# The reciprocal root of the norms on GpSimd instead of VectorE, in a hybrid encoder block on one core

## The chip, the cores and the metric

The kernel runs on one core of one Trainium2 chip. The metric is the device time of one execution in microseconds (us); lower is better. A core has five engines that run side by side, each with its own queue that is worked off in order: TensorE (PE in the profile; PEld is its loading of weights), VectorE (DVE), ScalarE (ACT), GpSimd (POOL) and SyncE (SP, which here only issues DMAs). They wait for each other through semaphores.

## The reference, cut to what matters

One layer of a streaming encoder on a sequence of 256 tokens with 1024 channels, all in float32:

```
x <- x + 1/2 * rmsnorm(swiglu(rmsnorm(x)))          first FFN, 2816 wide
h  = rmsnorm(x);  p = h @ w_in                      one projection, split into
A  = HGRN2 recurrence (8 heads), then rmsnorm and an output gate
B  = forgetting attention (8 heads, causal)
y  = gate_A * (A @ w_branch_a) + gate_B * (B @ w_branch_b)
x <- x + rmsnorm(y @ w_out)
x <- x + rmsnorm(cross_attention(rmsnorm(x), rmsnorm(mem)))     4 heads, 256 memory rows
x <- x + 1/2 * rmsnorm(swiglu(rmsnorm(x)))          second FFN

def rmsnorm(x, g):
    y = x * rsqrt(mean(x * x, axis=-1) + EPS)
    return y * g
```

What matters here is the `rsqrt` in `rmsnorm`: one number for each token, ten norms, each over two halves of 128 tokens.

## The kernel before, in words

The 256 tokens are two halves `h` of 128, one token to a partition. All matrix products keep float32 precision by splitting each operand into a high part `hi` (rounded to the format that TensorE takes) and a low part `lo`, and adding three products. The weights are 260 units of 128 x 1024. For each unit (function `unit`, lines 118 to 120) SP loads `raw`, ScalarE makes `hi` (L119) and VectorE makes `lo = raw - hi` (L120). There are 4 buffers for `raw` and 8 each for `hi` and `lo`, so the units are prepared ahead of their use. Every product is recorded by the helper `MM`, so all of them have line L78.

A norm is computed in three steps. ScalarE sums the squares of a row in two halves of 512 columns (`ssq`, L235). `rstd_of` turns the two sums into the reciprocal root. It does so without a table: a first value from the bits of the number taken as an integer (L221), then three Newton steps of two instructions (L224 and L226), and, if `scaled`, a last factor (L231). All its operands are 128 x 1. The result is then used in one of these ways:

- `post` adds a normed output to `x`. For one half: `ssq` on the two PSUM banks, L292 (the bank times the gain, into `post`), `rstd_of` without the last factor, and L296 (`xs = post * root + xs`). In the last FFN the two DMAs of the output half follow.
- `half` transposes the new `x` of a half for the next stage (`to_T`: transposes on PE at L269, then ScalarE L260 and VectorE L261), and calls `rstd_x`, which gives the root of the new `x`. The root is applied later, after the product, so PE need not wait for it.
- `row_of` makes a row of 256 roots: VectorE multiplies the identity with the root (L252, `diag`), PE multiplies it with ones, ScalarE copies the row (L255). VectorE then multiplies product banks with that row (L307 and L309 in the FFNs).
- The root of a half is also a factor in L443, L601, L602, L641, L729, L315, L317 and others.

`rstd_of` is called 20 times: two for each of the five norms on entry to a stage (four of `x`, one of `mem`), two for the norm behind HGRN2 (L641 uses it), and eight in `post`.

The order of the work on each engine is set when the program is built: a planner orders the instructions by priority, from the order in which they are written and from its own costs. `after(i)` gives a block a high priority and queues its instructions behind the `i`-th product. The constants L_F1, L_IA, L_WO, L_MK, L_MO and L_F2 place the transposes of `half` in this way.

GpSimd does little: the identity, some memsets, two selects (L651), and the DMAs of L208, L210, L467, L645 and L649 in its queue.

Of the kernel before, what the change touches and what calls it, by code (L numbers as in the profile page):

```python
# [11 lines left out]
I32 = mybir.dt.int32  # L12
AF = mybir.ActivationFunctionType
ALU = mybir.AluOpType
# [3 lines left out]
D = 1024  # L18
# [5 lines left out]
EPS = 1e-6  # L24
# [39 lines left out]
def block_kernel(ctx: ExitStack, tc: tile.TileContext, wts, x_in, xT_in, mem_in, memT_in, cols, rows, fbias, masks, out):  # L64
    nc = tc.nc
    V, S, G, PE = nc.vector, nc.scalar, nc.gpsimd, nc.tensor
# [21 lines left out]
    def nm(s):  # L88
        count[0] += 1
        return f"{s}_{count[0]}"  # L90

    def m4(shape, dt=F32, n="m"):
        return mp.tile(shape, dt, tag="m4", name=nm(n))

    def s1(n=1, dt=F32, name="s"):
        return sp.tile([P, n], dt, tag=f"s{n}", name=nm(name), bufs=16)
# [119 lines left out]
    def rstd_of(s, scaled=True):  # L216

        v = s1(name="v")
        V.tensor_scalar(out=v, in0=s[:, 0:1], scalar1=s[:, 1:2], scalar2=D * EPS, op0=ALU.add, op1=ALU.add)
        y = s1(name="y")  # L220
        V.tensor_scalar(out=y.bitcast(I32), in0=v.bitcast(I32), scalar1=-0.5, scalar2=1597463007.0, op0=ALU.mult, op1=ALU.add)  # L221
        for c in (3.0, 12.0, 768.0):
            t = s1(name="t")
            V.scalar_tensor_tensor(out=t, in0=v, scalar=y, in1=y, op0=ALU.mult, op1=ALU.mult)  # L224
            y2 = s1(name="y")
            V.scalar_tensor_tensor(out=y2, in0=t, scalar=c, in1=y, op0=ALU.subtract, op1=ALU.mult)  # L226
            y = y2
        if not scaled:
            return y
        r = s1(name="rstd")  # L230
        V.tensor_scalar(out=r, in0=y, scalar1=-1.0 / 256.0, scalar2=None, op0=ALU.mult)  # L231
        return r

    def ssq(dst, src):
# [2 lines left out]
    def rstd_x(src):  # L237

        s = s1(2, name="ss2")
        for j in range(2):  # L240
            ssq(s[:, j : j + 1], src[j])
        return rstd_of(s)
# [42 lines left out]
    def post(ps, h, grow, factor=1.0, last=False):  # L285

        s = s1(2, name="ss2")
        ts = []
        for j in range(2):
            ssq(s[:, j : j + 1], ps[j])  # L290
            t = sp.tile([P, 512], F32, tag="z2", name=nm("post"), bufs=3)
            V.scalar_tensor_tensor(out=t, in0=ps[j], scalar=-factor / 256.0, in1=grow[:, j * 512 : (j + 1) * 512], op0=ALU.mult, op1=ALU.mult)  # L292
            ts.append(t)
        r = rstd_of(s, scaled=False)
        for j, (t, xh) in enumerate(zip(ts, x_halves(h))):
            V.scalar_tensor_tensor(out=xh, in0=t, scalar=r, in1=xh, op0=ALU.mult, op1=ALU.add)  # L296
            if last:
                nc.sync.dma_start(out[h * P : (h + 1) * P, j * 512 : (j + 1) * 512], xh)
# [307 lines left out]
    for c in range(2):  # L606
        for name, lst, sc in (("k_b", kb_, 1.0), ("q_b", qb_, 1.0 / math.sqrt(128.0))):
            u = chunk(name, c)
            t = m4([P, 4, T], n=name)
# [20 lines left out]
    for h in range(2):  # L630
# [8 lines left out]
        r = rstd_x(ps)  # L639
# [7 lines left out]
    for g in range(2):  # L647
        t = m4([P, 4, T], n="cbm")
# [74 lines left out]
    for c in range(2):  # L723
        u = chunk("v_b", c)
        t = m4([P, 2, 512], n="v_b")
# [86 lines left out]
    for c in range(2):  # L812
        u = chunk("mk", c)
        KM.more()
        for j in range(2):
            js = slice(2 * j, 2 * j + 2)
            ps = proj_col2(M, u, (2 * j, 2 * j + 1))
            t = sp.tile([P, 2, T], F32, tag="z2", name=nm("km"), bufs=3)
# [171 lines left out]
```

## Time and profile before

| what | us |
|---|---|
| median of three runs | 815.56 |
| lowest and highest of them | 814.79 and 817.03 |
| the profiled execution | 814.88 |
| its span in the profile | 813.1 |
| TensorE busy | 799.4 |
| VectorE busy | 538.7 |
| ScalarE busy | 409.7 |
| GpSimd busy | 10.2 |

The span runs from the first to the last recorded instruction. The time of the profiled execution is 1.8 us longer, for what lies around the span. The granted clock of TensorE was 0.998 of full speed. Times within the kernel are given from the start of the span. A line of the timeline reads: start, length, engine, source line, operation, output and inputs with their shapes, count, and in brackets the idle time of the engine before it and what ended that.

### The profile page before, as it was taken

To read this page: it belongs to the slowest core of one execution; us is meant where nothing else is said; L and a number is where in the kernel's file an instruction comes from. 1 tells how busy PE (TensorE), PEld (TensorE's weight loads), DVE (VectorE), ACT (ScalarE), POOL (GpSimd) and SP (SyncE) were. 2 spreads that over 40 slices of the span, in tenths; PEclk is the share of its full clock that TensorE was granted. 3 is DMA by queue.
4 is the path that set the end of the run, shared out by engine and by line. 5 is a ranking of instruction groups with operands and counts; after the bars stand their busy time and mean duration, and the time that the engine had idled before them with its cause. 6 is when DMAs were issued, how large, how long until landed. Compare 5 with 4: busy or idle time off the path is not lost.

```text
span 813.1 us, 15302 instructions
## 1 busy us (share of the span) xinstructions
PE 799.4 (98%) x6292; PEld 743.5 (91%) x6292; DVE 538.7 (66%) x866; ACT 409.7 (50%) x621; POOL 10.2 (1%) x22
## 2 busy tenths in 40 slices
PE   8999999999999999999999999999999999999996
PEld 8999999997799889998999998999887899999994
DVE  6964666468776896678585556975748654665454
ACT  7644544436664435348675335744647544444431
POOL 0000000000000100100000000000000000000000
PEclk9999999999999999999999999999999999999999
DMA  8874466464564454543477446456426664566421
GB/s 322 256 264 156 163 207 226 157 207 160 171 208 170 149 193 161 198 152 121 139 231 243 150 168 220 156 179 203 143 83 197 208 207 156 164 212 227 149 104 52
DMA packets 41093, 147.02 MB, mean 181 GB/s; under 512 B 4744, under 2 KB 4752, under 8 KB 41024
## 3 DMA queue, kind: packets, MB, share of 16 engines
q1 hardware_dynamic: 40320, 144.20, 52.3%
q0 software_dynamic: 560, 1.81, 0.7%
q8 instruction: 49, 0.80, 0.4%
q14 instruction: 20, 0.16, 0.1%
q10 hardware_dynamic: 144, 0.04, 0.0%
HBM read 144.97 MB, written 1.06 MB: 180 GB/s over the span
## 4 chain that ended last, share of the span: by engine, by line
PE 92%; DVE 4%; DMA 2%; issue 1%; ACT 1%; DVEq 0%; ACTq 0%
PE mm L78 66%; PE acc L78 22%; PE tr L78 2%; DVE lo L120 1%; DMA raw<-in_wts_dram 1%; DVE xs L296 1%; PE tr L269 1%; ACT junk L235 1%; DVE t L224 1%; DMA cols_s<-in_cols_dram 0%; DVE y L226 0%; DVE post L292 0%; PE tr L697 0%; ACT hT L260 0%; PE tr L867 0%
## 5 line engine op out<-in xcount | busy, mean ns | idle before, releaser
L120 DVE TENSOR_TENSOR lo<-raw,hi 128x1024 fp32r<-128x1024 f32 (+1 forms) x262 | 315.5, 1221 | 134.3 <-ACT hi L119 131.8
L78 PE MATMUL mm<-hT,hi 128*128 128x256 f32 x1240 | 351.3, 283 | 0.0
L78 PE MATMUL mm<-lT,hi 128*128 128x256 f32 x1240 | 351.2, 283 | 0.0
L78 PE MATMUL mm<-hT,lo 128*128 128x256 f32 x1240 | 351.1, 283 | 0.0
L119 ACT CAST hi<-raw 128x1024 fp32r<-128x1024 f32 (+1 forms) x262 | 263.5, 1045 | 132.8 <-PE mm L78 87.9
L78 PEld LDWEIGHTS mm<-lT,hi 128*128 128x128 f32 x1240 | 237.9, 192 | 0.7
L78 PEld LDWEIGHTS mm<-hT,hi 128*128 128x128 f32 x1240 | 237.9, 192 | 0.6
L78 PEld LDWEIGHTS mm<-hT,lo 128*128 128x128 f32 x1240 | 237.8, 192 | 0.1
L78 PE MATMUL acc<-hi,act 128*128 128x512 f32 x352 | 111.4, 390 | 0.0
L78 PEld LDWEIGHTS acc<-hi,act 128*128 128x128 f32 x352 | 66.2, 188 | 13.4
L78 PE MATMUL acc<-lo,act 128*128 128x512 f32 x176 | 68.7, 390 | 0.0
L78 PE MATMUL mm<-hi,hT 128*128 128x512 f32 x160 | 63.1, 395 | 0.0
L78 PE MATMUL mm<-hi,lT 128*128 128x512 f32 x160 | 63.0, 394 | 0.0
L78 PE MATMUL mm<-lo,hT 128*128 128x512 f32 x160 | 62.8, 394 | 0.0
L309 DVE TENSOR_TENSOR z<-mm,row 128x512 f32<-128x512 f32 x36 | 24.8, 689 | 39.0 <-PE mm L78 39.0
L334 ACT ACTIVATE z<-z 128x512 f32<-128x512 f32 x20 | 12.6, 631 | 73.5 <-DVE z L309 73.4
L78 PEld LDWEIGHTS acc<-lo,act 128*128 128x128 f32 x176 | 33.1, 188 | 6.2
L78 PEld LDWEIGHTS mm<-hi,hT 128*128 128x128 f32 x160 | 30.1, 188 | 6.5 <-ACT hT L260 0.7
L78 PEld LDWEIGHTS mm<-hi,lT 128*128 128x128 f32 x160 | 30.1, 188 | 6.4 <-DVE lT L261 0.3
L78 PEld LDWEIGHTS mm<-lo,hT 128*128 128x128 f32 x160 | 30.1, 188 | 5.8
L292 DVE SCALAR_TENSOR_TENSOR post<-acc,grow 128x512 f32<-128x512 f32 x16 | 11.0, 690 | 30.1 <-ACT junk L235 29.6
L235 ACT ACTIVATE junk<-acc 128x512 f32<-128x512 f32 x20 | 12.0, 600 | 35.9 <-PE acc L78 35.6
(195 smaller groups left out, 703.4 us busy)
## 6 DMA issues: line engine op xcount, KB each, us to landing
raw<-in_wts_dram SPq DMA_DIRECT2D x260, 512.0 KB, 4.5
grow<-in_rows_dram SPq DMA_DIRECT2D x4, 512.0 KB, 5.9
xT<-in_xT_dram SPq DMA_DIRECT2D x4, 256.0 KB, 5.5
xs<-in_x_dram SPq DMA_DIRECT2D x2, 512.0 KB, 7.8
cbm<-cd POOLq DMA_DIRECT2D x2, 512.0 KB, 6.6
memT<-in_memT_dram SPq DMA_DIRECT2D x2, 512.0 KB, 6.9
ms<-in_mem_dram SPq DMA_DIRECT2D x2, 512.0 KB, 6.5
out_dram<-xs SPq DMA_DIRECT2D x4, 256.0 KB, 2.0
```

Of the source, the lines that this page charges most:

```text
L78: log.append(PE.matmul(*args, **kw).ins)
L119: S.copy(hi[:, cut], raw[:, cut])
L120: V.tensor_tensor(out=lo[:, cut], in0=raw[:, cut], in1=hi[:, cut].bitcast(F32), op=ALU.subtract)
L224: V.scalar_tensor_tensor(out=t, in0=v, scalar=y, in1=y, op0=ALU.mult, op1=ALU.mult)
L235: S.activation(junk[:, : src.shape[-1]], src, AF.Square, accum_out=dst)
L269: PE.transpose(ps[:, j * P : (j + 1) * P], src(kb), ident)
L292: V.scalar_tensor_tensor(out=t, in0=ps[j], scalar=-factor / 256.0, in1=grow[:, j * 512 : (j + 1) * 512], op0=ALU.mult, op1=ALU.mult)
L296: V.scalar_tensor_tensor(out=xh, in0=t, scalar=r, in1=xh, op0=ALU.mult, op1=ALU.add)
L309: V.tensor_tensor(out=z, in0=ps, in1=bc(row, [P, 2, T], 1), op=ALU.mult)
L334: S.activation(z[:, 0], z[:, 0], AF.Silu)
```

## The change

Inside `rstd_of`, all instructions are issued on GpSimd (`G`) instead of VectorE (`V`). The two instructions of a Newton step take another form for that: `scalar_tensor_tensor`, with one scalar and two tensors, becomes `tensor_scalar` with two scalar operands, the second of which is the 128 x 1 tile. The numbers of instructions stay: 8 in a call without the last factor, 9 with it. Nothing else in the program is touched.

```diff
     def rstd_of(s, scaled=True):
         v = s1(name="v")
-        V.tensor_scalar(out=v, in0=s[:, 0:1], scalar1=s[:, 1:2], scalar2=D * EPS, op0=ALU.add, op1=ALU.add)
+        G.tensor_scalar(out=v, in0=s[:, 0:1], scalar1=s[:, 1:2], scalar2=D * EPS, op0=ALU.add, op1=ALU.add)
         y = s1(name="y")
-        V.tensor_scalar(out=y.bitcast(I32), in0=v.bitcast(I32), scalar1=-0.5, scalar2=1597463007.0, op0=ALU.mult, op1=ALU.add)
+        G.tensor_scalar(out=y.bitcast(I32), in0=v.bitcast(I32), scalar1=-0.5, scalar2=1597463007.0, op0=ALU.mult, op1=ALU.add)
         for c in (3.0, 12.0, 768.0):
             t = s1(name="t")
-            V.scalar_tensor_tensor(out=t, in0=v, scalar=y, in1=y, op0=ALU.mult, op1=ALU.mult)
+            G.tensor_scalar(out=t, in0=v, scalar1=y, scalar2=y, op0=ALU.mult, op1=ALU.mult)
             y2 = s1(name="y")
-            V.scalar_tensor_tensor(out=y2, in0=t, scalar=c, in1=y, op0=ALU.subtract, op1=ALU.mult)
+            G.tensor_scalar(out=y2, in0=t, scalar1=c, scalar2=y, op0=ALU.subtract, op1=ALU.mult)
             y = y2
         if not scaled:
             return y
         r = s1(name="rstd")
-        V.tensor_scalar(out=r, in0=y, scalar1=-1.0 / 256.0, scalar2=None, op0=ALU.mult)
+        G.tensor_scalar(out=r, in0=y, scalar1=-1.0 / 256.0, scalar2=None, op0=ALU.mult)
         return r
```

## The prediction

> **What bounds the kernel now.** I read the page's busy times first, then the busy time by stretches, then what TensorE (PE) waits for, and last the timeline where the moved work's results are awaited.
>
> ```profile
> PE 799.4 (98%) x6292; PEld 743.5 (91%) x6292; DVE 538.7 (66%) x866; ACT 409.7 (50%) x621; POOL 10.2 (1%) x22
> ```
>
> PE is busy for all but 13.7 us of the 813.1 us span. The stretches (start:end, length, then busy time of PE, weight load, VectorE (DVE), ScalarE (ACT), GpSimd (POOL)) show where those lie:
>
> ```profile
> 0.00:20.00 20.00, 16.51 (x110) 16.21 (x111) 13.12 (x38) 14.47 (x27) 1.90 (x8) 1.00 0.88 327
> 20.00:184.00 164.00, 164.00 (x1176) 155.32 (x1175) 99.99 (x114) 74.20 (x84) 0.00 (x0) 1.00 0.59 203
> 184.00:212.00 28.00, 26.88 (x124) 21.34 (x123) 23.81 (x66) 19.12 (x42) 0.00 (x0) 1.00 0.47 151
> ...
> 600.00:640.00 40.00, 39.23 (x182) 31.39 (x181) 32.30 (x78) 26.93 (x52) 0.00 (x0) 1.00 0.45 141
> ...
> 800.00:813.10 13.10, 5.06 (x23) 3.85 (x21) 4.21 (x12) 1.38 (x4) 0.00 (x0) 0.85 0.14 52
> ```
>
> Idle PE: 3.5 us at the start (before any norm), 8.0 at the end, 1.1 and 0.8 at the two FFN seams, 0.2 elsewhere. So a lighter VectorE is worth nothing in itself. What can count is the latency of a norm's chain, from its last sum of squares (ACT, L235) to the use of the root, where PE waits for it or the end does. PE's waits name such places:
>
> ```profile
> PE tr L269 <- DVE xs L296: 1.1, 2, 0.9
> PE tr L323 <- DVE at L317: 0.5, 1, 0.5
> ```
>
> **What moves.** `rstd_of` runs 20 times: 8 instructions in the eight `post` calls, 9 in the other twelve. Their groups on VectorE (count | busy us, mean ns | idle before):
>
> ```profile
> L224 DVE SCALAR_TENSOR_TENSOR t<-v,y 128x1 f32<-128x1 f32 x60 | 13.1, 218 | 1.4
> L226 DVE SCALAR_TENSOR_TENSOR y<-t,y 128x1 f32<-128x1 f32 x60 | 9.5, 158 | 1.5
> L219 DVE TENSOR_SCALAR v<-ss 128x1 f32<-128x1 f32 x20 | 4.1, 207 | 4.1 <-ACT junk L235 4.1
> ```
>
> With L221 (3.0 us) and L231 (1.8), 172 instructions and 31.5 us leave VectorE. By the argument above that is booked at nothing: PE hides it, and only chains count. Counts stay equal, so the change cannot be empty: all 172 come back on POOL, and the loop carries each result into the next.
>
> **The price of one POOL instruction in a chain.** None of this form is in the trace. The nearest rows:
>
> ```profile
> L980 POOL MEMSET const-float32-1.0<- 128x1 f32 x1 | 0.1, 108 | 0.0
> masks.py:199 POOL TENSOR_SCALAR_AFFINE_SELECT ident<-ident 128x128 f32<-128x128 f32 x1 | 0.3, 313 | 0.1
> ...
> 325.86 1.09 POOL L651 TENSOR_SCALAR_AFFINE_SELECT cbm<-cbm 128x1024 f32<-128x1024 f32 x1 [4.82 <-DMA cbm<-cd]
> 328.01 1.89 POOL L651 TENSOR_SCALAR_AFFINE_SELECT cbm<-cbm 128x1024 f32<-128x1024 f32 x1 [1.06 <-DMA cbm<-cd]
> ```
>
> The memset writes only: 0.11 us, and the memsets at 281 to 284 us stand 0.06 apart, so the low end is 0.17. The select reads as well: 0.313 us for 128 columns and 1.087 for 1024 make 0.86 ns a column and 0.20 fixed. With the gap of 0.06 that is 0.26; with the 0.29 us that passed between the end of the scan L465 on DVE (231.17) and POOL's DMA behind it (231.46), it is 0.49, the high end. The new instructions read up to two scalar operands beside the input, and each needs the result before it, so I take a value nearer the high row: **0.40 us** a step, 3.2 for eight and 3.6 for nine, where VectorE takes 1.77 (806.53 to 808.30) and 1.95.
>
> **Contention.** The second select took 1.89 us, not 1.09. Beside it on VectorE:
>
> ```profile
> 327.72 3.25 DVE L120 TENSOR_TENSOR lo<-raw,hi 128x1024 fp32r<-128x1024 f32 x2 [3.85 <-ACT hi L119]
> ```
>
> Two L120 take 2.35 us elsewhere and 3.25 here; before them VectorE was idle for 3.85 us, so the first select met no work there. Each made the other wait. Once moved, a step that starts while an L120 runs waits for the rest of it, 0.6 us of 1.22 on average. I charge 0.6 for each L120 that falls into a chain; L120 fills 315.5 of the 813.1 us.
>
> The Trainium skill, "SBUF — State Buffer", section "Who interferes with whom", says that a VectorE instruction with two SBUF inputs and a GpSimd instruction that reads SBUF exclude each other for the whole instruction; the 1.89 us agrees.
>
> **Place by place** (each against the times of this profile).
>
> The end: the last sum is ready at 805.88, but `v` started at 806.53 because VectorE was still in L292. POOL can start at 805.95 and ends at 809.15, plus 0.05 to return: L296 starts at 809.2, not 808.30. No L120 runs here. **+0.9**.
>
> The start: two chains of nine feed `row_of` (r1). The second diagonal (L252) is ready at 22.23 now, and PE takes it at 22.32 without waiting, with all of chunk 1 queued behind it. On POOL: 15.95 + 18 x 0.40 = 23.15, and 0.3 for hop and L252, gives 23.45: 1.2 later. Three L120 fall in (ACT has their input ready at 18.3, 19.3 and 20.6): 1.8. PE has no idle time from 20 to 184 to absorb it. **+3.0**.
>
> The HGRN2 norm (354.83 on): nine steps, one L120 (354.99) inside: 354.85 + 3.6 + 0.6 = 359.05, and with the return 359.1 to 359.4 against 357.84 for L641, which frees the banks that the score matmuls enter at 358.83, a few tenths behind it. +1.3; the second half's chain starts at 358.02, queues behind it and ends about 0.2 late. **+1.5**.
>
> The seams: `post`, then transposes L269 wait for L296. Today two L120 are interleaved into those chains on VectorE, and at 201.65 and 620.15 the chain also stands behind the other half's root, starting only at 204.42 and 622.92. POOL starts it at once. With eight steps and two L120 (1.2) a chain lasts 4.4: 201.65 to 206.1 (now 206.27), 504.35 to 508.75 (508.78), 604.7 to 609.1 (609.17), 620.15 to 624.55 (624.77). **-0.4** in all. While L296 waits in VectorE's queue, the L120 behind it wait too; eight `hi`/`lo` buffers at 3.1 us of PE time per unit (799 us for 260) cover a few us; without that cover it would be a PE stall of the same length.
>
> Roots with slack are booked at nothing: r2 (diagonal at 212.03, PE at 221.21), mem (417 to 425, used at 486). POOL's own queue holds no chain behind its long waits (232 to 281, 284 to 320): no root is computed between 212 and 354. No DMA moves.
>
> Sum: 0.9 + 3.0 + 1.5 - 0.4 = **+5.0**. The profiled execution took 814.88 (its span 813.1 and 1.8 around it), so 819.9; from the median of 815.56, which is 0.7 higher, it would be 820.6. I keep 819.9.
>
> **Rivals.** *Cheap step, same contention* (0.26): the end -0.2, the start 15.95 + 4.7 + 1.8 + 0.3 = 22.75 or +0.5, HGRN2 0, and the seams' chains become 3.3, which removes PE's 1.1 and 0.8 us of idle: -1.9. Sum -1.6: **813.3**, no change that can be told. For it: the select's row. Against it: two scalar reads and a dependence at every step.
>
> The Trainium skill, "GPSIMD Engine Reference", section "Performance pitfalls for Q7 kernels", gives about 102 cycles for each small read command; at the 1.2 GHz that it states, 18 reads in eight steps are an estimated 1.5 us, some 2.4 with eight memset spans, and the sum would then lie near this rival; no run here shows the reads alone.
>
> *Faster: the queue was the cost.* At 0.17 a step and no L120 in the way, the chain takes 1.4 us: the end gains 1.0 and the seams 2.1 (all their idle): **811.8**. It decides below 0.29 a step, where the end breaks even ((808.30 - 805.95 - 0.05) / 8). Against it stands the doubled L120 row.
>
> *Dear step* (0.49 and beyond): the end +1.6, the start +1.6 more than forecast, HGRN2 +2.3, the seams' four chains +0.7 each less 0.4; sum 4.6 + 1.6 + 2.3 + 2.4 = +10.9: **825.8**. At 0.6 the same arithmetic gives above 830.
>
> *The order shifts.* The planner places PE's transposes and row product by its own price for POOL. If it takes POOL for cheap, PE stands in order at each of them; that is priced within the dear case.
>
> **How the numbers follow.** Forecast (+5.0) 0.43; cheap step 0.28; faster 0.12; dear 0.17. A difference under 0.3% (2.4 us) is about what a measurement of this kernel cannot tell from none, so faster 0.12, same 0.28, slower 0.60. The range takes in the cheap case and the high row with its error: 812.8 to 829; its slower cases alone span 818 to 829.
>
> **What would show it.** Right: POOL about 172 instructions busier, with starts 0.35 to 0.45 us apart in the last chain; L296 starting 3.3 us after the last sum; a PE wait of some 3 us at the diagonal product around 22 us; VectorE near 507 us busy. Wrong: spacing under 0.29 in the last chain; no PE wait near 22 us; L120 keeping 1.22 us beside POOL's steps; or a PE wait at the seams above 2 us each, which would make the order and not the step the cause.

## The result and the profile after

The changed kernel takes 844.66 us (844.20 to 845.38) where the kernel before, on the same chip, took 815.3: a ratio of 1.036 (95% interval 1.0347 to 1.0372), 29 us slower. The forecast was 819.9 with a range up to 829.0, so the sign was right, several terms came out near, and the size was far off. The profiled execution took 844.2, with a span of 842.4.

The busy times of the page:

```profile
PE 809.8 (96%) x6292; PEld 748.9 (89%) x6292; DVE 514.3 (61%) x694; ACT 409.2 (49%) x621; POOL 67.9 (8%) x194
```

The 172 instructions moved as written. Of the 29.3 us by which the span grew, PE idles 18.9 (842.4 less 809.8 is 32.6, it was 13.7), and for 10.4 PE is busier with the same 6292 matmuls, so they ran slower. Both have to be found. What PE waits for (line, releaser: us in total, times, longest):

```profile
PE tr L323 <- DVE at L317: 4.0, 1, 4.0
PE tr L269 <- DVE lT L261: 3.6, 2, 3.1
PE tr L269 <- DVE xs L296: 3.1, 4, 1.5
...
PE mm L78 <- ACT hT L260: 2.3, 2, 1.2
PE tr L78 <- DVE diag L252: 2.2, 2, 1.9
PE acc L78 <- DVE G L641: 2.0, 2, 1.6
```

The diagonal (2.2) and L641 (2.0) are places that the prediction named. The first four lines lie in the seams, where it had booked a small gain. A seam is the stretch in which one stage's norm ends and the next stage's first products begin: here FFN1's (184 to 220 us), w_out's (500 to 540) and mo's (600 to 660). Behind them stands VectorE, and VectorE stands for GpSimd:

```profile
DVE diag L252 <- POOL rstd L231: 27.5, 8, 6.5
DVE xs L296 <- POOL y L226: 20.2, 8, 3.0
```

The windows of the first seam and of the last one (start:end, length, busy time of PE, PEld, DVE, ACT, POOL, granted clock, DMA share, GB/s). In the first, PE was busy for 34.88 of the 36 us before, with VectorE at 30.33:

```profile
184.00:220.00 36.00, 32.02 (x134) 24.34 (x134) 19.89 (x34) 18.83 (x42) 10.34 (x34) 0.95 0.38 127
600.00:660.00 60.00, 53.53 (x251) 43.01 (x250) 31.96 (x49) 29.68 (x59) 10.37 (x34) 0.94 0.32 106
```

PE and VectorE are both less busy, and the clock is below 1. The timeline shows why. First the seam behind FFN1 before:

```profile
187.45 1.22 DVE L120 TENSOR_TENSOR lo<-raw,hi 128x1024 fp32r<-128x1024 f32 x1
188.92 1.22 DVE L120 TENSOR_TENSOR lo<-raw,hi 128x1024 fp32r<-128x1024 f32 x1
190.06 1.41 DVE L296 SCALAR_TENSOR_TENSOR xs<-post,y,xs 128x512 f32<-128x512 f32 x2
```

and the same place after:

```profile
191.83 1.41 DVE L296 SCALAR_TENSOR_TENSOR xs<-post,y,xs 128x512 f32<-128x512 f32 x2 [2.48 <-POOL y L226]
193.17 2.43 DVE L120 TENSOR_TENSOR lo<-raw,hi 128x1024 fp32r<-128x1024 f32 x2
198.88 0.29 DVE L252 TENSOR_SCALAR diag<-ident,rstd 128x128 f32<-128x128 f32 x1 [3.28 <-POOL rstd L231]
```

Before, the planner let two L120 go ahead of L296, between the steps of the root. After, L296 is queued first, VectorE stands 2.48 us, and the same two L120 come behind it. The diagonal L252, whose product PE takes up much later, is queued right behind the root too, and VectorE stands 3.28 us more, with L120 and L261 behind it. At the last seam it meets PE directly:

```profile
651.94 0.22 POOL L231 TENSOR_SCALAR rstd<-y 128x1 f32<-128x1 f32 x1
652.19 0.29 DVE L252 TENSOR_SCALAR diag<-ident,rstd 128x128 f32<-128x128 f32 x1 [3.29 <-POOL rstd L231]
652.39 0.48 DVE L317 SCALAR_TENSOR_TENSOR at<-mm,rstd,sg 128x256 f32<-128x256 f32 x1
652.92 0.44 PE L323 MATMUL tr<-ident,at 128*128 128x128 f32 x2 [3.95 <-DVE at L317]
```

Comparing the start of the n-th matmul in both traces places the whole loss: start of the kernel +3.0, FFN1's seam +5.5, the stretch around 305 us +1.6, HGRN2 norm +2.5, w_out's seam +6.0, mo's seam +9.6, last outputs +0.8 (and some 0.3 in between).

The end went as forecast. The last root on GpSimd:

```profile
834.49 0.29 POOL L219 TENSOR_SCALAR v<-ss 128x1 f32<-128x1 f32 x1 [7.85 <-ACT junk L235]
...
836.84 0.34 POOL L224 TENSOR_SCALAR t<-v,y 128x1 f32<-128x1 f32 x1
837.28 0.29 POOL L226 TENSOR_SCALAR y<-t,y 128x1 f32<-128x1 f32 x1
```

Eight instructions start from 834.49 to 837.28, seven distances of 0.40 on average; from the last sum to L296 it is 3.21 us, 2.42 before.

### The profile page after: what moved, and what is told of

It reads as the page before. It is cut to its first block, busy times and chain, and to the rows that moved or that the text cites. A ratio compares the mean times of both kernels' runs of the same rounds, so it can differ in the third digit from the quotient of the medians.

```text
span 842.4 us, 15347 instructions
## 1 busy us (share of the span) xinstructions
PE 809.8 (96%) x6292; PEld 748.9 (89%) x6292; DVE 514.3 (61%) x694; ACT 409.2 (49%) x621; POOL 67.9 (8%) x194
## 3 DMA queue, kind: packets, MB, share of 16 engines
HBM read 144.97 MB, written 1.06 MB: 173 GB/s over the span
## 4 chain that ended last, share of the span: by engine, by line
PE 86%; POOL 5%; issue 2%; DMA 2%; ACT 2%; DVE 2%; SPq 0%; DVEq 0%; POOLq 0%; ACTq 0%
PE mm L78 64%; PE acc L78 19%; POOL t L224 2%; POOL y L226 2%; PE tr L78 2%; ACT junk L235 1%; DMA raw<-in_wts_dram 1%; DMA xs<-in_x_dram 1%; PE tr L269 1%; POOL v L219 1%; DVE xs L296 1%; ACT hi L119 1%; DMA cols_s<-in_cols_dram 0%; DVE lo L120 0%; POOL y L221 0%
## 5 line engine op out<-in xcount | busy, mean ns | idle before, releaser
L120 DVE TENSOR_TENSOR lo<-raw,hi 128x1024 fp32r<-128x1024 f32 (+1 forms) x262 | 314.6, 1219 | 136.6 <-ACT hi L119 134.8
L78 PE MATMUL mm<-hi,hT 128*128 128x512 f32 x160 | 65.1, 407 | 2.3 <-ACT hT L260 2.3
L78 PE MATMUL mm<-lo,hT 128*128 128x512 f32 x160 | 64.5, 403 | 0.0
L219 POOL TENSOR_SCALAR v<-ss 128x1 f32<-128x1 f32 x20 | 8.4, 420 | 638.0 <-ACT junk L235 638.0
L260 ACT ACTIVATE hT<-tr,cols_s 128x128 fp32r<-128x128 f32 x64 | 21.0, 366 | 17.9 <-DVE lT L261 14.5
```

The source lines that it names most:

```text
L78: log.append(PE.matmul(*args, **kw).ins)
L120: V.tensor_tensor(out=lo[:, cut], in0=raw[:, cut], in1=hi[:, cut].bitcast(F32), op=ALU.subtract)
L219: G.tensor_scalar(out=v, in0=s[:, 0:1], scalar1=s[:, 1:2], scalar2=D * EPS, op0=ALU.add, op1=ALU.add)
L260: S.activation(X.hi(kb, a, b), src, AF.Copy, scale=gs)
```

## The experiments

All kernels of an experiment are compared with the kernel before on the same chip; the brackets hold the ratio to it and its 95% interval. "Slip" is how much later the n-th matmul starts than in the kernel before.

**1. Which roots?** The eight roots of `post` alone on GpSimd, and the twelve others alone.

```diff
     def rstd_of(s, scaled=True):
+        E = V if scaled else G      # e1_post_pool; the other way round in e2_entry_pool
```

> Only the eight chains of post run on GpSimd, the twelve entry roots on VectorE. Theory Q (queue order: the planner counts GpSimd as nearly free and puts the VectorE instruction that needs the root too early, VectorE stands there, in the changed kernel 20.2 us at L296, 27.5 at L252, 4.5 at L641, 1.4 at L847, and the L120 and L261 behind it come late): only the 20.2 us at L296 stay, 20.2/53.6 of 29.4 us, so about 826 us (821 to 831). Theory L (latency alone: a chain is 1.6 us longer, and that counts only where PE or the end waits for the result, which is after post): nearly all of the loss stays, 836 to 844. Theory C (GpSimd and VectorE exclude each other at their SBUF interface, loss by the number of GpSimd steps, 64 of 172): 826.

> The complement: the twelve entry roots on GpSimd, post on VectorE. Theory Q: the 33.4 us of standing at L252, L641 and L847 stay, so about 833 us (827 to 838). Theory L: the start (+3.0) and HGRN2 (+1.5) alone, about 820. Theory C: 108 of 172 steps, about 834.

Measured: 827.87 (1.0150, 1.0124 to 1.0175) and 827.47 (1.0153, 1.0137 to 1.0168). The two losses are about equal and add to 25 of the 29 us. In e1 the slip at the three seams is 4.1, 1.6 and 4.7; in e2 it is 1.5, 0.2 and 2.7, the start takes 4.5 and the HGRN2 norm 3.4. Theory Q is the only one of the three that has both times in its ranges, the second at the very edge. So neither kind of root carries the loss alone, and at w_out's seam the two together (6.0) cost far more than one by one (1.8). In e1 VectorE's waits for a root are these:

```profile
DVE xs L296 <- POOL y L226: 17.1, 7, 2.6
```

**2. Is it VectorE standing at L252?** Two ways to take waits there away: the diagonal goes to GpSimd, or it stays on VectorE but is queued behind the last L120 that the program has written before it.

```diff
-            V.tensor_scalar(out=dg, in0=ident, scalar1=r2[h], scalar2=None, op0=ALU.mult)
+            G.tensor_scalar(out=dg, in0=ident, scalar1=r2[h], scalar2=None, op0=ALU.mult)   # e3_diag_pool
+            with tc.issue_after(los[-1]): V.tensor_scalar(...)                             # e4_diag_late
```

> The changed kernel with L252 (identity times root) on GpSimd too; PE, ScalarE and SyncE keep their order, VectorE loses only the eight L252. Theory Q: the 27.5 us of standing at L252 go, some 15 of the 29.4 us with them: 828 to 834 us, no wait of VectorE for L231 at L252. Theory L: the chains are as long as before, 844 to 846. Theory C: eight more GpSimd instructions, 845.

> The changed kernel with each L252 left on VectorE, but queued behind the last L120 written before it; the order of the other four engines does not change. Theory Q: VectorE no longer stands at L252 except at the start (about 5 us stay): 829 to 835 us. Theory L and theory C: no change, 844 to 845.

Measured: 841.11 (1.0321, 1.0306 to 1.0337) and 841.24 (1.0323, 1.0307 to 1.0338). Both give back 3.5 us, less than theory Q expected and more than the other two. They get there in different ways. In e3 all 27.5 us are gone; the stretch around 305 us, mo's seam and FFN1's come back by 1.6, 3.9 and 1.3 us, but the start slips by 6.9 instead of 3.0, because the diagonal takes 0.62 us on GpSimd and one step of the root now stands beside an L120 and takes 1.38. In e4 less than expected goes away:

```profile
DVE diag L252 <- POOL rstd L231: 12.4, 4, 3.7
```

So 15.1 us of waiting less were worth 3.5 us, and at mo's seam L317 still stands behind L252 there (3.20 us). Most of what VectorE waited at L252 was idle time that nobody needed; how much of the rest counts is not shown.

**3. Does the length of the root matter, and on which engine?** The third step left out on GpSimd, a fourth step on GpSimd, and a fourth step on VectorE.

```diff
-        for c in (3.0, 12.0, 768.0):
+        for c in (3.0, 12.0):                          # e5_two_steps, of the changed kernel
+        for c in (3.0, 12.0, 768.0, 201326592.0):      # e8_pool_four, of the changed; e6_dve_four, of the one before
```

> The changed kernel with the third of the three steps left out (6 or 7 GpSimd instructions in a root instead of 8 or 9; what it leaves out is the last refinement of the root; the constants are rescaled to match). The order of the instructions on TensorE, VectorE and ScalarE stays that of the changed kernel but for one matmul at the start. By the 0.41 us between two steps a root takes 0.82 us less, so about as long as on VectorE before (2.42 us from the last sum to L296). Theory L (each seam loses what its serial roots are late, whatever the order): the seams come back nearly whole, and the start, the HGRN2 norm and the end lose half of theirs: 818 to 824 us. Theory O (the planner's order, in which VectorE and ScalarE and TensorE stand in front of L296 and of what follows it, is the cost): the order is unchanged, only the start (1.6), the HGRN2 norm (1.6) and the end (0.8) give back: 838 to 841 us.

> The changed kernel with a fourth step (two more GpSimd instructions, 0.82 us more in each root; the value is the same). Theory L (latency): as much again at every root as the change cost over the kernel before: 866 to 874 us. Theory O (the order, which changes little): the start 1.6, the HGRN2 norm 1.6 and the end 0.8 more, and a us or two at the seams: 848 to 853 us.

> The kernel before, with a fourth step (two more instructions of some 0.3 us on VectorE in each of the 20 roots; the value is the same). No root runs on GpSimd. Each root is some 0.6 us longer in latency, on VectorE. Theory L (latency alone, on any engine): the 28 us that 0.8 us a root cost in the changed kernel, times 0.6 over 0.8: 833 to 838 us. Theory O (crossing to another engine and the order made for it): VectorE works through other things between the steps, the end loses 0.6 and the start 1.2, little else: 817 to 820 us.

Measured: 831.51 (1.0187, 1.0172 to 1.0202), 857.09 (1.0501, 1.0486 to 1.0517) and 815.31 (0.9992, 0.9982 to 1.0001). On GpSimd two instructions more or less in each root change the time by 13.2 and 12.4 us, 0.8 us for each us that the twenty roots grow (20 times 0.82). On VectorE two instructions more, in the order that the planner made for them, cost nothing. Neither theory had both: L expected 818 to 824 for the short roots and 833 to 838 for the long ones on VectorE; O expected 838 to 841 for the short ones, and 857.09 lies between what the two expected for the long ones on GpSimd. At the three seams together the slip is 21.0 us in the changed kernel, 11.8 in e5 and 28.5 in e8.

What differs is the order. Leaving the third step out on GpSimd moved one matmul in the whole built program, which suggests that the planner hardly prices a step there. With a fourth step on VectorE, 110 of PE's instructions and 33 of VectorE's beside the roots stand in another place in the trace than in that of the kernel before (with the change itself 144 and 52; places are compared in the order of starts, by line, operation and tiles). That the planner made room for the longer roots with other work is a reading of this and not shown by itself.

**4. Is it the order?** First PE's transposes are held back by six constants to about where they stood before (those of w_out's first half still come 4 to 5 places early); the planner moves some of the other work with them.

```diff
-L_F1 = 18 ... L_IA = 22 ... L_WO = 18 ... L_MK = 46 ... L_MO = 18 ... L_F2 = 44
+L_F1 = 27 ... L_IA = 38 ... L_WO = 34 ... L_MK = 92 ... L_MO = 26 ... L_F2 = 45     # e7_late_pe
```

> The changed kernel with six constants raised (L_F1 27, L_IA 38, L_WO 34, L_MK 92, L_MO 26, L_F2 45), so that TensorE's transposes of the residual stand in its order where they stood in the kernel before (5 to 46 instructions later at the seams), and what VectorE and ScalarE do on their results too. The roots stay on GpSimd. Theory L (each seam loses what the roots are late): the transposes find xs ready, but what follows waits as long: 842 to 846 us. Theory O (standing in the planner's order is the cost): TensorE's waits at L269 (6.7 us) and the half-clock stretches behind them go: 832 to 838 us.

Measured: 836.22 (1.0249, 1.0225 to 1.0272): 8.4 us come back, some of the loss but not the most. Then the orders of the two built programs were written out and exchanged. `_STAND` lists an engine's instructions in the wanted order, and each gets an edge, for order only and without a wait, to the one ahead of it.

```diff
+    named = {i.name: i for i in nc.cur_bb.bb.instructions}
+    for engine, text in _STAND.items():
+        stand(engine, text)     # tc.add_manual_dep(this, the one ahead of it, NoSync)
```

In e9_all_order the changed kernel gets the order of the kernel before on PE, ScalarE and VectorE; in e13_dve_after_order the kernel before gets that of the changed one; e10_dve_order and e11_pe_order restore it in the changed kernel on a single engine. The traces of e9 and e13 show the wanted order on all three engines in every place.

> The changed kernel (every root on GpSimd), with the order of the instructions on TensorE, ScalarE and VectorE written out by ordering edges so that it is that of the kernel before in every place; only the roots' own instructions are gone from VectorE. Theory O (the order that the planner made for the changed kernel carries the loss at the seams): what stays is the start (3.0), the HGRN2 norm (1.5 to 2.5), the end (0.8) and little at the seams: 818 to 824 us. Theory L (a root on GpSimd is late for VectorE's queue in any order): 835 to 845 us.

> The reverse: the kernel before (every root on VectorE), with the order of the instructions on TensorE, ScalarE and VectorE written out so that it is that of the changed kernel; each root stands on VectorE just ahead of what needs it. Nothing runs on GpSimd that did not before. Theory O (order): VectorE does not stand but works at the root in the same place, TensorE still stands at transposes that come early: 828 to 840 us. Theory L (the wait for another engine): 814 to 819 us.

> The changed kernel with the order written out on VectorE alone, as in the kernel before; TensorE's and ScalarE's stay with the planner, which moves them nearly back too (two fifths of the differences stay). If VectorE's order carries the loss: 820 to 826 us, as with all three written out. If TensorE's and ScalarE's places carry it: 828 to 836 us.

> The changed kernel with the order written out on TensorE alone, as in the kernel before; VectorE's and ScalarE's stay with the planner (most of their differences stay). If TensorE's places carry the loss: 820 to 826 us. If VectorE's queue carries it (L296 and L252 ahead of the L120): 832 to 838 us, near the 836.2 that the six constants gave.

| median us, beside the kernel before | order of before | order of the changed kernel |
|---|---|---|
| roots on VectorE | 815.4 | 831.58 (1.0195, 1.0181 to 1.0209) |
| roots on GpSimd | 822.76 (1.0086, 1.0069 to 1.0103) | 844.66 (1.0360, 1.0347 to 1.0372) |

The order alone costs 16 us with every root still on VectorE, its steps just ahead of what needs them. GpSimd alone, in the old order, costs 7. The 6 that are left come only with both. Theory O's ranges hold in e7, e9 and e13. PE's largest waits in the seams of e13 are those of the changed kernel, nearly as long, without a root on GpSimd:

```profile
PE tr L323 <- DVE at L317: 3.3, 1, 3.3
PE tr L269 <- DVE lT L261: 2.9, 1, 2.9
PE tr L269 <- DVE xs L296: 2.7, 1, 2.7
```

while in e9, with all roots on GpSimd, these are the largest, but for one of 2.4 us at the very start that the kernel before has too. The first stands for one wait of about 1 us at each seam, the last for the diagonal of the first norm:

```profile
PE tr L269 <- DVE xs L296: 3.1, 3, 1.1
...
PE tr L78 <- DVE diag L252: 2.0, 1, 2.0
```

The length of the root fits in: with short roots on GpSimd, about as long as on VectorE, and with the changed order, e5 gave 831.5, beside e13's 831.6. That the two are equal is in part chance: the start slips by 1.5 in e5 and not at all in e13, FFN1's, w_out's and mo's seam by 3.6, 2.0 and 6.3 against 4.4, 5.7 and 3.8. That in this order only the place and the length of a root count, and not its engine, is therefore not shown.

On a single engine: VectorE's order restored gives 828.02 (1.0147, 1.0127 to 1.0167), 16.6 us back; TensorE's gives 842.59 (1.0328, 1.0305 to 1.0351), 2 us. The first lies outside the range that stood for VectorE's order alone and at the edge of the other, the second outside both of its ranges. The two engines are not separated by this: with VectorE's order written out the planner moved PE's back as well (37 of the 144 differences are left), while with PE's written out 47 of VectorE's 52 stayed. What can be said is that PE's order gains little as long as VectorE's is the new one. PE then waits for the L120 themselves (4.3 us in e11, none in the changed kernel). Why e11 gains less than e7, whose transposes stand nearly in the same places, is left open.

**5. Where are the 7 us of the old order, and is there a better one?** In e14_some_pool six roots (first norm, HGRN2 norm, last outputs) go back to VectorE, fourteen stay on GpSimd, in the old order. e15_dve_order6 is the kernel before with the order that the planner had made for four steps.

```diff
     def rstd_of(s, scaled=True):
+        E = G if next(seq) in (2, 3, 4, 5, *range(8, 18)) else V     # e14_some_pool
```

> The order of the kernel before written out on TensorE, ScalarE and VectorE; six of the twenty roots (the two of the first norm, the two of the HGRN2 norm, the two of the last outputs) stay on VectorE, the fourteen others run on GpSimd. Theory A (what is left of the loss when the order is kept, 7 us, lies where TensorE waits for a root with nothing else to do: start 4.0, HGRN2 norm 1.4, end 0.8, w_out 0.9, FFN1's seam -0.9): 814.5 to 816.5 us. Theory B (it is spread over all roots, as contention or as VectorE standing at L296 and L252): 818 to 820 us.

> The kernel before (three steps, all on VectorE), with the order written out that the planner made for the four steps (e6_dve_four), the fourth step's places left out. If that order is by itself the better one (its records ran 1.2 us ahead of the kernel before by the mo projection, in spite of longer roots): 813.6 to 814.8 us. If the 1.2 us belong to that one execution: 815.0 to 816.0 us.

Measured: 816.48 against 816.32 (0.9999, 0.9987 to 1.0011) and 813.36 (0.9960, 0.9947 to 0.9972). The 7 us lie in the six roots that PE or the end waits for; fourteen roots on GpSimd cost nothing, within 1 us, when the order is kept. The best kernel of the study, faster than both, moves no root at all: it is the kernel before in an order made for roots of two more instructions, a little below the lower of the two expected ranges. In that same order the longer roots of e6 stand at 0.9992. By the two ratios, taken on different chips, the two instructions cost some 2.6 us there, which suggests that e6 cost nothing because the order that came with them was the better one, and not because VectorE does them for free. The trace of e15 has a span of 812.0 with PE busy for 799.4, so PE waits 1.1 us less; the seams' waits at L269 and L323 that the prediction showed (1.1 and 0.5) are no longer in its list. The spans of e6 and e15 are 812.3 and 812.0. The rest of the 3 us between the medians is not seen in the traces.

## Why the prediction was wrong

- **The price of a step.** Forecast 0.40 us, measured 0.40. Right, though it was a choice between two rows at 0.26 and 0.49, so the exact hit is luck. The end followed from it, +0.9 forecast and +0.8 measured. The cheap case (0.26), and with it the estimate of 1.5 us for 18 reads from the Trainium skill, "GPSIMD Engine Reference", "Performance pitfalls for Q7 kernels", had eight steps in 2.4 us and the end 0.2 earlier; they took 3.1 (834.49 to 837.57), and the trace does not agree.
- **The start.** Forecast +3.0, measured +3.0, and that is luck. The sum was 1.2 for the steps and 1.8 for three L120 inside the chain. No L120 fell in, because VectorE stood at both diagonals, and the second was ready at 22.98, only 0.75 later than before:

```profile
19.34 0.32 DVE L252 TENSOR_SCALAR diag<-ident,rstd 128x128 f32<-128x128 f32 x1 [3.75 <-POOL rstd L231]
22.69 0.29 DVE L252 TENSOR_SCALAR diag<-ident,rstd 128x128 f32<-128x128 f32 x1 [3.04 <-POOL rstd L231]
22.89 1.22 DVE L120 TENSOR_TENSOR lo<-raw,hi 128x1024 fp32r<-128x1024 f32 x1
23.03 0.49 PE L78 MATMUL tr<-diag,ones 128*128 128x128 f32 x2 [1.88 <-DVE diag L252]
```

PE waited 1.88 us for it, where the prediction looked for some 3, and 0.37 for the first, because the new order has the second product 21 matmuls earlier; 0.6 us more were late at 12 us, before any norm. In e9, with the old order, two L120 do fall in (two steps take 1.06 and 1.20 us), the diagonal is 2.7 later, and the start costs +4.0: 2.0 of waiting at the diagonal and then 3.4 us at half the clock.
- **The HGRN2 norm.** Forecast +1.5, measured +2.5, of which the order brings 1.5 (e13); in e9, with the old order, it is +1.4. The +1.6 around 305 us, booked at nothing, goes with the order too: 1.3 in e13, none in e9.
- **The seams.** Forecast -0.4, measured +21.1. This is the step that failed. It took each chain's steps out of VectorE's row and left every other instruction where the trace of before had it. (Its four differences add to 0.5, not 0.4.) In that order the forecast was near: in e9 the seams slip by -0.9, +0.7 and 0.1, where the -0.9 and the +0.7 all but cancel, and with the start, the norm and the end its span grows by 6.2 (the medians by 7.4), against the forecast's 5.0. What was forecast was e9, whose 822.76 lies in the range, and not the changed kernel. But the order is made anew when the program is built. The planner put L296 and L252 ahead of the L120 that had stood in front of them, and the transposes up to 46 places earlier on PE. That order alone cost 16.2 us (e13), 13.9 of them at the seams.
- **The cover.** "Eight `hi`/`lo` buffers [...] cover a few us" was the sentence that made VectorE's standing harmless. It holds for most of the waiting at L252 (15.1 us less of it, 3.5 us of time, e4). It does not hold at the seams, where roots 0.82 us shorter or longer each take 9.2 us off or put 7.5 on (e5, e8). Why is argued from the code and not tried by itself: there both halves run over the same eight units, so all eight come free only in the second pass, just when VectorE stands.
- **The rival.** *The order shifts* named the mechanism, and the last sentence of "what would show it" its sign, PE waits above 2 us at the seams. But it was "priced within the dear case", at 825.8, without an own sum. A bound was at hand in the prediction's own terms: VectorE standing for a whole chain of 3.2 us at each of the six L296 of the seams is an estimated 19 us, where the dear case charged the seams 2.4. Measured were 20.2 us at the eight L296 of all `post` calls.
- **Contention.** Forecast 0.6 us for each L120 in a chain. In the changed kernel GpSimd met few of them, because VectorE stood: `t` takes 369 ns on average. In e9 VectorE worked on, and `t` takes 514:

```profile
L224 POOL TENSOR_SCALAR t<-v,y 128x1 f32<-128x1 f32 x60 | 30.8, 514 | 6.0
```

```profile
626.24 1.22 DVE L120 TENSOR_TENSOR lo<-raw,hi 128x1024 fp32r<-128x1024 f32 x1
626.37 1.34 POOL L224 TENSOR_SCALAR t<-v,y 128x1 f32<-128x1 f32 x1
```

The step, which takes 0.34 us when it has no L120 beside it, takes 1.34 and ends 0.25 us behind the L120: it waited for the L120's end, as the prediction had it, and the L120 lost nothing. The Trainium skill, "SBUF — State Buffer", "Who interferes with whom", excludes the two for the whole instruction; this row agrees.

- **VectorE's busy time.** Forecast 507, measured 514.3. The 31.5 us that were taken off are a sum of durations that overlap on VectorE; the busy time fell by 24.4.

## What to carry to other kernels

Where a planner orders the queues, moving an operation to another engine changes the order of everything around it; write that order out (or count, at each place, what now stands behind the waiting instruction) before summing latencies. Exchanging the orders of two kernels, with edges that carry no wait, separates the engine from the order in two runs. A wait at the head of an in-order queue costs what is queued behind it and not its own length: taking away 15.1 us of waiting at L252 (e4) was worth 3.5, while 17.1 us at L296 (e1) went with 12.8.

## What the hardware showed

At four places in the seams PE's granted clock was about one half for 3.4 us, each time behind a stretch in which PE was in part idle. At the first seam (start:end, length, PE busy, granted clock, DMA share, GB/s):

```profile
202.80:206.20 3.40, 1.69 (x6) 1.00 0.90 302
206.20:209.60 3.40, 3.40 (x9) 0.51 0.67 227
209.60:213.00 3.40, 1.88 (x11) 0.99 0.40 139
213.00:216.40 3.40, 3.40 (x18) 1.00 0.44 123
```

Behind 3.4 us with PE busy half of the time, the next 3.4 us run at a clock of 0.51, and matmuls start 0.43 us apart instead of 0.23:

```profile
206.62 0.63 PE L78 MATMUL mm<-lo,hT 128*128 128x512 f32 x1
207.04 0.63 PE L78 MATMUL mm<-hi,lT 128*128 128x512 f32 x1
```

So here a stall of some 1.7 us was paid twice. In the 3.4 us ahead of the other three places (from 530.5, 636.3 and 650.0 us) PE was busy for 0.76, 2.20 and 0.48 us. How little is too little can't be read from this: the stretch from 209.60, with 1.88 us, was followed by a full clock. Four windows of 12 us behind the three seams show a mean clock of 0.86, some 1.7 us lost in each and 6.7 of the 10.4 us that PE was busier. Where the other 3.7 us went is left open. The slow stretches go with the stalls: PE is busy for 804.6 us in e13 and 800.6 in e9. The Trainium skill, "TensorE: Matmul & The Clock Gate", "What's actually happening", tells of a clock halved after an idle window of about 3.4 us and restored after a busy one; the lengths agree, but here PE was half busy in the stretch before 206.20, not idle.
